# SBUF offsets of streamed matrix operands: halves of gated values at 128 bytes, the last attention group's operands at 64

## The chip, the cores and the metric

The kernel runs on one core of one Trainium2 chip. The metric is the device time of one execution in microseconds. Three executions of the kernel before took 2158.36, 2160.70 and 2164.97 us. One more execution was profiled; it took 2162.09 us, of which 2160.3 us lie between its first and its last instruction.

In the text PE is TensorE's multiplication, PEld its loading of the stationary operand, DVE is VectorE, ACT ScalarE, POOL GpSimd, and SP the engine that issues most DMAs. "Line 2125" or L2125 is a line of the kernel's source. SBUF is the on-chip memory of 128 partitions; an address in it is a number of bytes within each partition.

## The reference

One layer of a hybrid encoder over 2048 prompt tokens and 64 sample tokens, in fp32. Cut to what matters here:

```python
D_MODEL, SEQ, DEC_SEQ, D_FF, N_HEADS, HEAD_DIM = 1024, 2048, 64, 2816, 4, 128

def layer(x, ...):
    h = rmsnorm(x, g1) * (1 + sc1) + sh1
    u, q, k, v, o, gates = split(h @ w_in)          # one combined input projection
    pool_out = pool_mixer(u, ...)                   # causal pooling in 4 channel groups
    hs = mlstm_seq(q, k, v, gates, ...)             # matrix memory, 4 heads, chunks of 64
    x = x + gt1 * (concat([pool_out, gated(hs, o)]) @ w_out)
    h2 = rmsnorm(x, g2) * (1 + sc2) + sh2
    up = h2 @ w_up                                  # 1024 -> 2 x 2816
    conv = b_conv + sum(w_conv[j] * shifted(up, j) for j in range(3))
    a, g = split(conv)
    x = x + gt2 * ((silu(g) * a) @ w_down)          # 2816 -> 1024
    return x, new states
y = rmsnorm(x, g_final)
```

## The kernel before

**Arithmetic.** Every large product is made of three passes in fp32r: an operand is split into a high part (an ACT copy that rounds) and a low part (a DVE subtraction), and `PASSES` runs high x high, high x low and low x high. Values of a tile lie as `[128, 2, columns]`: the high part, then the low part. The stationary operand of a product is a block of 128 columns of a weight tile `wt`; the moving operand is a stretch of tokens. TensorE loads a stationary block before each multiplication.

**Attention part.** The 2112 tokens run in four groups of 512; the last has 576, since it takes the 64 sample tokens with it. Its normalized input is in eight tiles `hl`, the mixed output of the heads and the pooling in eight tiles `mx`. `gemm` (line 496) streams them against the weights of q, k, o, u and of the output projection: one multiplication of 512 columns for the first three groups, two of 256 and 320 columns for the last (`o.blks`). For v (line 1171) the roles are turned: blocks of `hl` are stationary and the weights move.

**Feed-forward part.** Three token groups of 704 columns (`FT`), each handled as two halves of 352 (`FH`). The up projection (line 1633) uses a scheme with seven products of half-sized blocks instead of eight; its moving operands are sums of input blocks in tiles `hx`. A pair of output rows is convolved and gated, and the gated values go to the down projection in one of two ways:

- four rows at a time through the same scheme (`Quad`, `quad_down`, line 2125): seven operands named B11, B21, B22, T1, T2, T3, T4, each half a group wide, two of them to a tile `av`. B21 with B22 and T2 with T3 are split together, 704 columns at once (`wide_hi`, line 1858 on ACT; `wide_lo`, line 1861 on DVE); the others are split alone, 352 columns at once;
- six rows plainly (`down`, line 2271): a tile `av` holds one row of 704 gated values (`split_hi`, `split_lo`), streamed as 448 and 256 columns (`ENDS`).

There are seven buffers for `av` (`AVB`); the tiles `qs`, in which weight blocks are added up, share them.

**Where the tiles lie.** Pools are stacked in SBUF from both sides, so a tile's address follows from the sizes of all that lie outside of it. All weight blocks start at a multiple of 256 bytes. In the program as built the moving operands start this far past a multiple of 256 bytes:

| Operand | Line | Columns | Bytes past |
|---|---|---|---|
| hl, mx, first three groups | 496 | 512 | 0 |
| hl, mx, last group | 496 | 256 and 320 | 128 |
| hx | 1633 | 352 | 128 |
| av, halves for quad_down | 2125 | 352 | 32 or 160 |
| av, full rows | 2271 | 448 and 256 | 160 |

For `hl` the tile's length is 18.5 times 256 bytes, so tiles start at 0 and 128 in turn, and `taken` counts along to move the operands in every second one. The stationary blocks of `hl` at line 1171 lie at 0 in the first three groups and at 128 in the last.

**Other tiles.** `fscr` gives scratch tiles of one row of 704: under the tag "rb" the row by which a normalization multiplies, under "ssum" the running sum of squares; each tag has one buffer. `final_end` finishes the last tokens; its tile `rs` is the last small one of the pool that also holds `av` and the residual rows `x0` to `x7`.

**What sets the order.** In the feed-forward part the instructions of TensorE, ACT, DVE and POOL run in the order in which the Python code issues them. Background work is cut into steps of generators (`bg`, `tick`) that are taken between multiplications; tiles are handed out in turn, and a first write into a buffer waits until the last reader of its former content is done.

Of the kernel before, what the change touches and what calls it, by code (L numbers as in the profile page):

```python
# [9 lines left out]
F32 = mybir.dt.float32  # L10
F32R = mybir.dt.float32r
AF = mybir.ActivationFunctionType
# [4 lines left out]
P = 128  # L17
# [6 lines left out]
TMAX = GT + TS  # L24
NF = 22
FT = 704
# [41 lines left out]
def tile_layer(ctx: ExitStack, tc: tile.TileContext, xT, vecs, cst, rst, w_mod, w_ada, w_qkou, w_v, w_pool,  # L68
# [73 lines left out]

    def two_parts(t, past):

        return t[:, 32 * past:32 * past + 2 * TMAX].rearrange("p (a t) -> p a t", a=2)

    def hl_tile(k, o=None):

        taken.append(1 - taken[-1])
        return two_parts(hp.tile([P, 2 * TMAX + 32], F32R, tag="hl", name=f"hl{k}"), taken[-2] ^ (o is not None and o.last))  # L150

    def mx_tile(k, o=None):
        return two_parts(mx.tile([P, 2 * TMAX + 64], F32R, tag="mx", name=f"mx{k}"), o is not None and o.last)

    x0, c0 = [[t[:, i * GT:(i + 1) * GT] for t in [big(mx_tile(k)) for k in range(4)] for i in range(2)] for _ in range(2)]

# [525 lines left out]

    def fscr(dt=F32):
        if dt in ("rb", "ssum"):
            return spare[0].tile([P, FT], F32, tag=dt, name=dt)
        return spare[0].tile([P, FT], dt, tag="fscr", name="fscr", bufs=4)


# [994 lines left out]
    def quad_sums(ds, lead=7):  # L1683

        for d in ds:
            for c in (0, 256):
                t = f2.tile([P, 2, FT], F32R, tag="av", name="qs", bufs=AVB)
                w = t.bitcast(F32).rearrange("p a t -> p (a t)")[:, :1024].rearrange("p (i c) -> p i c", i=4)
                nc.sync.dma_start(out=w, in_=w_quad[d, :, :, c:c + 256])
                for _ in range(lead):  # L1690
                    yield
                a11, a12, a21, a22 = (w[:, i] for i in range(4))
                dve.tensor_tensor(out=a22, in0=a21, in1=a22, op=ALU.add)
                yield
                dve.tensor_tensor(out=a21, in0=a11, in1=a21, op=ALU.subtract)
                yield
                dve.tensor_tensor(out=a11, in0=a22, in1=a11, op=ALU.subtract)
                yield
                dve.tensor_tensor(out=a12, in0=a12, in1=a11, op=ALU.subtract)
                yield  # L1700
                yield
                nc.sync.dma_start(out=dsum[d, :, :, c:c + 256], in_=w)
                yield
                yield

    def half_tile(nm):
        return f1.tile([P, FH], F32, tag=nm, name=nm)

    class Quad:

# [4 lines left out]
        def put(self, nm, m, part):  # L1715
            key, at = {"B11": (("a", m), 0), "T1": (("a", m), 1), "B21": (("b", m), 0), "B22": (("b", m), 1),
                       "T2": (("c", m), 0), "T3": (("c", m), 1), "T4": ("d", m)}[nm]
            if key not in self.tiles:
                self.tiles[key] = f2.tile([P, 2, FT], F32R, tag="av", name="av", bufs=AVB)
            return self.tiles[key][:, part, at * FH:(at + 1) * FH]  # L1720

        def both(self, nm, m, part):
            self.put(nm, m, part)
            return self.tiles["b" if nm == "B21" else "c", m][:, part, :]

    class Pair:

# [127 lines left out]
            return self.quad.gated[self.m, i]  # L1855

        def wide_hi(self, nm, t):
            act.activation(self.quad.both(nm, self.m, 0), t[:, :FT], AF.Copy)

        def wide_lo(self, nm, t):  # L1860
            dve.tensor_tensor(out=self.quad.both(nm, self.m, 1), in0=t[:, :FT],
                              in1=self.quad.both(nm, self.m, 0).bitcast(F32), op=ALU.subtract)

        def step_2(self):
# [42 lines left out]
                self.lo("T4", self.blocks()[2])  # L1907

        def split_hi(self):
            self.d = self.d or f2.tile([P, 2, FT], F32R, tag="av", name="av", bufs=AVB)  # L1910
            for (a, b, s) in self.o.segs:
                act.activation(self.d[:, 0, a:b], self.tg[:, a + 2 * s:b + 2 * s], AF.Copy)
            self.av[self.i] = self.d
# [70 lines left out]
    def final_end(o, x3, sums, lo, hi):  # L1984
# [3 lines left out]
        for _ in range(YA if lo == 0 else 0):  # L1988
            yield
        ps = m2_ps()  # L1990
        rs = f2.tile([P, 5], F32, tag="rs", name="rs", bufs=1) if lo > 0 else RF
        if lo > 0:
            dve.memset(ps[:, :len(tiles)], 0.0)
            yield
# [442 lines left out]
```

## Time and profile before

| What | us |
|---|---|
| Median of three executions | 2160.70 |
| The profiled execution | 2162.09 |
| Its span, first to last instruction | 2160.3 |
| PE busy | 2142.7 |
| PEld busy | 2038.7 |
| DVE busy | 1650.1 |
| ACT busy | 1101.7 |
| POOL busy | 253.8 |

The busy time of PE includes the latency of multiplications that run one behind the other, so it says that there is always one under way, not how densely they follow. A row of a group gives the line, engine, operation, the program's names of the written and read tiles, shapes and count; then the busy time in us and the mean duration of one in ns; then the idle time of the engine ahead of these instructions, with what ended most of it. A row of a timeline gives start and length in us of a run of like instructions, from the first one's start to the last one's end, and their number. A row of windows gives a stretch, its length, then for PE, PEld, DVE, ACT and POOL the busy time with the number of instructions, the granted clock, the share of the DMA engines and GB/s.

### The profile page before, as it was taken

The page shows a single profiled execution, that of the slowest core. Times are in us where ns is not written, and L with a number is a line of the kernel's source. Part 1 is how long each engine was busy: PE and PEld are TensorE (multiplying, and loading weights), DVE is VectorE, ACT ScalarE, POOL GpSimd, SP SyncE. Part 2 cuts the span into 40 slices and gives each one's busy share as a digit, 9 for nine tenths or more (in the row PEclk, how much of TensorE's full clock was granted, in tenths as well). Part 3 has the DMA queues.
Part 4 walks back from the last instruction along what each step waited for, and adds up shares of the span by engine and source line. Part 5 has one row for each costly group of instructions (what it writes and reads, how often), then busy time and mean ns, then how long its engine had stood idle before and what let it go on. Part 6 is the DMA issues. An engine that isn't in the chain of part 4 may idle for free.

```text
span 2160.3 us, 38129 instructions
## 1 busy us (share of the span) xinstructions
PE 2142.7 (99%) x13556; PEld 2038.7 (94%) x13556; DVE 1650.1 (76%) x3060; ACT 1101.7 (51%) x2192; POOL 253.8 (12%) x470
## 2 busy tenths in 40 slices
PE   8999999999999999999999999999999999999998
PEld 7888888888899999999999999999999999999998
DVE  5777768678675779788688668988886597887875
ACT  4554335234323557465556445655655364564554
POOL 0010000001000301010001110100101221121112
PEclk9999999999999999999999999999999999999999
DMA  8987997898799588797669986665668675455442
GB/s 321 326 315 237 317 324 246 282 320 274 243 298 302 196 280 307 252 336 246 233 219 314 329 299 207 235 214 205 228 222 273 218 261 182 171 180 183 172 169 85
DMA packets 296839, 541.09 MB, mean 250 GB/s; under 512 B 25760, under 2 KB 112800, under 8 KB 296648
## 3 DMA queue, kind: packets, MB, share of 16 engines
q1 hardware_dynamic: 286600, 514.13, 69.9%
q10 hardware_dynamic: 10048, 24.51, 2.9%
q8 instruction: 107, 1.75, 0.3%
q14 instruction: 84, 0.69, 0.1%
HBM read 412.56 MB, written 125.98 MB: 249 GB/s over the span
## 4 chain that ended last, share of the span: by engine, by line
PE 89%; DVE 5%; DMA 3%; issue 1%; ACT 1%; SPq 0%; POOL 0%; DVEq 0%; ACTq 0%; POOLq 0%
PE mm L1633 35%; PE mm L496 24%; PE mm L2271 10%; PE mm L2125 10%; PE mm L1171 3%; DVE wt L432 1%; DMA wt<-wsum 1%; PE m L1361 1%; PE m L1383 1%; PE m L1381 1%; PE m L1346 1%; DMA w<-w_ada 1%; DVE x L2094 1%; DVE tg L1611 1%; ACT tg L1606 0%
## 5 line engine op out<-in xcount | busy, mean ns | idle before, releaser
L1633 PE MATMUL mm<-hx,wt 128*128 128x352 f32 x5544 | 888.8, 321 | 2.2 <-DVE wt L432 1.3
L1633 PEld LDWEIGHTS mm<-hx,wt 128*128 128x128 f32 x5544 | 881.0, 188 | 4.5 <-DVE wt L432 3.2
L496 PE MATMUL mm<-hl,wt 128*128 128x512 f32 (+2 forms) x1920 | 385.3, 356 | 0.0
L432 DVE TENSOR_TENSOR wt<-raw,wt 128x512 fp32r<-128x512 f32 (+1 forms) x460 | 310.4, 681 | 75.0 <-ACT wt L429 74.9
L496 PEld LDWEIGHTS mm<-hl,wt 128*128 128x128 f32 x1920 | 314.8, 188 | 46.8 <-issue 3.6
L429 ACT ACTIVATE wt<-raw 128x512 fp32r<-128x512 f32 (+1 forms) x460 | 274.1, 603 | 163.3 <-PE mm L496 53.9
L2125 PE MATMUL mm<-av,wt 128*128 128x352 f32 x1512 | 247.4, 323 | 1.4 <-DVE x L2094 0.7
L2125 PEld LDWEIGHTS mm<-av,wt 128*128 128x128 f32 x1512 | 242.3, 188 | 4.0 <-DVE wt L432 2.0
L2271 PE MATMUL mm<-av,wt 128*128 128x448 f32 (+1 forms) x1440 | 231.3, 322 | 0.0
L2271 PEld LDWEIGHTS mm<-av,wt 128*128 128x128 f32 x1440 | 220.9, 188 | 9.7
L2094 DVE SCALAR_TENSOR_TENSOR x<-mm,MOD,x 128x352 f32<-128x352 f32 (+3 forms) x368 | 171.7, 507 | 73.3 <-PE mm L2271 58.3
L1681 ACT ACTIVATE mm<-mm 128x352 f32<-128x352 f32 x204 | 91.4, 448 | 240.9 <-PE mm L1633 177.1
L496 PE MATMUL mm<-mx,wt 128*128 128x512 f32 (+1 forms) x960 | 182.6, 352 | 0.0
L496 PEld LDWEIGHTS mm<-mx,wt 128*128 128x128 f32 x960 | 159.3, 188 | 22.5
L1611 DVE SCALAR_TENSOR_TENSOR ta<-ea,V,ta 128x704 f32<-128x704 f32 (+1 forms) x132 | 125.7, 952 | 61.3 <-ACT ta L1606 56.8
L1611 DVE SCALAR_TENSOR_TENSOR tg<-eg,V,tg 128x704 f32<-128x704 f32 (+1 forms) x132 | 125.7, 952 | 52.7 <-ACT tg L1606 50.2
L432 DVE TENSOR_TENSOR wt<-wt 128x512 fp32r<-128x512 f32 x204 | 138.8, 684 | 12.7 <-ACT wt L429 10.6
L429 ACT ACTIVATE wt<-wt 128x512 fp32r<-128x512 f32 x204 | 123.6, 621 | 31.3 <-DMA wt<-wsum 30.5
L1589 POOL COPY ea<-UC 128x2 f32<-128x2 f32 x66 | 34.7, 525 | 539.3 <-DVE ta L1611 425.3
L1829 ACT ACTIVATE tg<-tg 128x704 f32<-128x704 f32 (+1 forms) x66 | 52.5, 795 | 71.1 <-DVE tg L1611 71.1
L1171 PE MATMUL mm<-wt,hl 128*128 128x256 f32 (+1 forms) x576 | 71.2, 284 | 0.0
L1171 PEld LDWEIGHTS mm<-wt,hl 128*128 128x128 f32 x576 | 70.2, 189 | 0.8 <-issue 0.6
(315 smaller groups left out, 2204.4 us busy)
## 6 DMA issues: line engine op xcount, KB each, us to landing
wt<-wsplit SPq DMA_DIRECT2D x132, 512.0 KB, 4.3
raw<-w_up SPq DMA_DIRECT2D x198, 256.0 KB, 4.1
wt<-hl_kept SPq DMA_DIRECT2D x96, 512.0 KB, 6.0
wt<-wsum SPq DMA_DIRECT2D x132, 256.0 KB, 4.9
wsplit<-wt SPq DMA_DIRECT2D x66, 512.0 KB, 5.0
w<-w_up SPq DMA_DIRECT2D x88, 256.0 KB, 4.6
wsum<-w SPq DMA_DIRECT2D x44, 512.0 KB, 5.4
Bd<-fscr ACTq DMA_DIRECT2D x56, 352.0 KB, 3.9
```

Source lines behind the costliest of these rows:

```text
L429: act.activation(u.w[:, 0, :u.n], u.raw[:, :u.n], AF.Copy)
L432: dve.tensor_tensor(out=u.w[:, 1, :u.n], in0=u.raw[:, :u.n], in1=u.w[:, 0, :u.n].bitcast(F32), op=ALU.subtract)
L496: pe.matmul(ps[bi][:, :hi - lo], U[:, a, k % 4 * P:(k % 4 + 1) * P], mv[k][:, b, lo:hi], start=(at == 0 and pi == 0), stop=(k == order[-1] ...
L1171: pe.matmul(ps[ti][:n, :cols], h[4 * kh + k4][:, b, lo:lo + n], U[:, a, k4 % 2 * cols:(k4 % 2 + 1) * cols], start=(kh == 0 and k4 == 0 and ...
L1589: pool.tensor_copy(ext[:, 0:2], UC[:, f, :])
L1611: dve.scalar_tensor_tensor(out=t[:, :E], in0=ext[:, j:j + E], scalar=wc(j, f), in1=t[:, :E], op0=ALU.mult, op1=ALU.add)
L1633: pe.matmul(bk.t[:, :FH], U[:, a, kc * P:(kc + 1) * P], Bo.at(nm, kc, b), start=(first and kc == 0 and pi == 0), stop=(kc == 3 and pi == 2 ...
L1681: act.activation(to.t[:, :FH], bk.t[:, :FH], AF.Copy)
L1829: act.activation(self.tg[:, :E], self.tg[:, :E], AF.Silu)
L2094: dve.scalar_tensor_tensor(out=x3[n][:, a:b], in0=bk.t[:, a - lo:b - lo], scalar=gt2(n, s), in1=x3[n][:, a:b], op0=ALU.mult, op1=ALU.add)
L2125: pe.matmul(bk.t[:, :FH], U[:, a, c:c + P], quad.put(op, m, b), start=(first and m == 0 and pi == 0), stop=(m == 1 and pi == 2), skip_grou ...
L2271: pe.matmul(bks[i].t[:, :hi - lo], U[:, a, k % 4 * P:(k % 4 + 1) * P], av[k][:, b, lo:hi], start=(k == 0 and (a, b) == PASSES[0]), stop=(k ...
```

## The change

It moves operands to other addresses, and enlarges some tiles for it:

- `av` tiles become 2 x 768 columns (`HX`) instead of 2 x 704. A half starts 384 columns (1536 bytes) after the other, so both have the same place within 256 bytes. Full rows start 8 columns (32 bytes) into their part, and stay where they were within 256 bytes.
- The pool of `av` begins 32 bytes lower, because `rs` gets a second buffer that nothing else uses. With that the halves lie at 128.
- The 3584 bytes that the seven larger tiles need are partly had by giving "ssum" the tag, and so the one buffer, of "rb".
- `hl` and `mx` of the last attention group start 16 columns (64 bytes) into their tiles. For `hl` the tiles themselves still start at 0 and 128 in turn.
- The splits of B21 with B22 and T2 with T3 write, and read, two runs of 352 columns instead of one of 704.

| Operand | Bytes past a multiple of 256, before | now |
|---|---|---|
| hl, last group, moving and stationary | 128 | 64 or 192 |
| mx, last group | 128 | 64 |
| av, halves | 32 or 160 | 128 |
| av, full rows | 160 | 160 |
| hx; hl and mx of the other groups; weights | | the same |

No instruction is added, removed or moved on any engine. What changes in the order's rows is the form of the wide splits. On DVE, where the gated values of a block's second pair are split (tg is the gated value, ta its other factor, wt a weight tile being split), the kernel before has:

```order
L1837 TENSOR_TENSOR tg<-ta,tg 128x704
L1849 TENSOR_TENSOR tg<-tg 128x352 x2
L432 TENSOR_TENSOR wt<-wt 128x512
L1861 TENSOR_TENSOR av<-tg,av 128x704
L432 TENSOR_TENSOR wt<-raw,wt 128x512
L1611 SCALAR_TENSOR_TENSOR ta<-ea,V,ta 128x704 x2
L1861 TENSOR_TENSOR av<-tg,av 128x704
```

At the same place of the change stands:

```order
L1843 TENSOR_TENSOR tg<-ta,tg 128x704
L1855 TENSOR_TENSOR tg<-tg 128x352 x2
L432 TENSOR_TENSOR wt<-wt 128x512
L1867 TENSOR_TENSOR av<-tg,av 128x2x352
L432 TENSOR_TENSOR wt<-raw,wt 128x512
L1611 SCALAR_TENSOR_TENSOR ta<-ea,V,ta 128x704 x2
L1867 TENSOR_TENSOR av<-tg,av 128x2x352
```

Lines below the edits are six further down (1861 becomes 1867, 2125 becomes 2131, 2271 becomes 2277); the sequence is the same, and the two subtractions have two runs. The diff:

```diff
--- before.py
+++ after.py
@@ -142,15 +142,15 @@
 
     def two_parts(t, past):
 
-        return t[:, 32 * past:32 * past + 2 * TMAX].rearrange("p (a t) -> p a t", a=2)
+        return t[:, past:past + 2 * TMAX].rearrange("p (a t) -> p a t", a=2)
 
     def hl_tile(k, o=None):
 
         taken.append(1 - taken[-1])
-        return two_parts(hp.tile([P, 2 * TMAX + 32], F32R, tag="hl", name=f"hl{k}"), taken[-2] ^ (o is not None and o.last))
+        return two_parts(hp.tile([P, 2 * TMAX + 32], F32R, tag="hl", name=f"hl{k}"), 16 if o is not None and o.last else 32 * taken[-2])
 
     def mx_tile(k, o=None):
-        return two_parts(mx.tile([P, 2 * TMAX + 64], F32R, tag="mx", name=f"mx{k}"), o is not None and o.last)
+        return two_parts(mx.tile([P, 2 * TMAX + 64], F32R, tag="mx", name=f"mx{k}"), 16 if o is not None and o.last else 0)
 
     x0, c0 = [[t[:, i * GT:(i + 1) * GT] for t in [big(mx_tile(k)) for k in range(4)] for i in range(2)] for _ in range(2)]
 
@@ -682,7 +682,7 @@
 
     def fscr(dt=F32):
         if dt in ("rb", "ssum"):
-            return spare[0].tile([P, FT], F32, tag=dt, name=dt)
+            return spare[0].tile([P, FT], F32, tag="rb", name=dt)
         return spare[0].tile([P, FT], dt, tag="fscr", name="fscr", bufs=4)
 
 
@@ -1684,7 +1684,7 @@
 
         for d in ds:
             for c in (0, 256):
-                t = f2.tile([P, 2, FT], F32R, tag="av", name="qs", bufs=AVB)
+                t = gated("qs")
                 w = t.bitcast(F32).rearrange("p a t -> p (a t)")[:, :1024].rearrange("p (i c) -> p i c", i=4)
                 nc.sync.dma_start(out=w, in_=w_quad[d, :, :, c:c + 256])
                 for _ in range(lead):
@@ -1703,8 +1703,14 @@
                 yield
                 yield
 
+    def gated(name="av"):
+        return f2.tile([P, 2, HX], F32R, tag="av", name=name, bufs=AVB)
+
     def half_tile(nm):
         return f1.tile([P, FH], F32, tag=nm, name=nm)
+
+    def halves(t):
+        return t[:, :FT].rearrange("p (h t) -> p h t", h=2)
 
     class Quad:
 
@@ -1716,12 +1722,12 @@
             key, at = {"B11": (("a", m), 0), "T1": (("a", m), 1), "B21": (("b", m), 0), "B22": (("b", m), 1),
                        "T2": (("c", m), 0), "T3": (("c", m), 1), "T4": ("d", m)}[nm]
             if key not in self.tiles:
-                self.tiles[key] = f2.tile([P, 2, FT], F32R, tag="av", name="av", bufs=AVB)
-            return self.tiles[key][:, part, at * FH:(at + 1) * FH]
+                self.tiles[key] = gated().rearrange("p a (h t) -> p a h t", h=2)[:, :, :, :FH]
+            return self.tiles[key][:, part, at]
 
         def both(self, nm, m, part):
             self.put(nm, m, part)
-            return self.tiles["b" if nm == "B21" else "c", m][:, part, :]
+            return self.tiles["b" if nm == "B21" else "c", m][:, part]
 
     class Pair:
 
@@ -1855,10 +1861,10 @@
             return self.quad.gated[self.m, i]
 
         def wide_hi(self, nm, t):
-            act.activation(self.quad.both(nm, self.m, 0), t[:, :FT], AF.Copy)
+            act.activation(self.quad.both(nm, self.m, 0), halves(t), AF.Copy)
 
         def wide_lo(self, nm, t):
-            dve.tensor_tensor(out=self.quad.both(nm, self.m, 1), in0=t[:, :FT],
+            dve.tensor_tensor(out=self.quad.both(nm, self.m, 1), in0=halves(t),
                               in1=self.quad.both(nm, self.m, 0).bitcast(F32), op=ALU.subtract)
 
         def step_2(self):
@@ -1907,7 +1913,7 @@
                 self.lo("T4", self.blocks()[2])
 
         def split_hi(self):
-            self.d = self.d or f2.tile([P, 2, FT], F32R, tag="av", name="av", bufs=AVB)
+            self.d = self.d or gated()[:, :, 8:8 + FT]
             for (a, b, s) in self.o.segs:
                 act.activation(self.d[:, 0, a:b], self.tg[:, a + 2 * s:b + 2 * s], AF.Copy)
             self.av[self.i] = self.d
@@ -1988,7 +1994,7 @@
         for _ in range(YA if lo == 0 else 0):
             yield
         ps = m2_ps()
-        rs = f2.tile([P, 5], F32, tag="rs", name="rs", bufs=1) if lo > 0 else RF
+        rs = f2.tile([P, 5], F32, tag="rs", name="rs", bufs=2) if lo > 0 else RF
         if lo > 0:
             dve.memset(ps[:, :len(tiles)], 0.0)
             yield
```

## The prediction

> **What bounds the kernel now.** I read the page's header and busy shares first, then its chain of waits, then the groups of the matrix engine with shapes kept apart.
>
> ```profile
> span 2160.3 us, 38129 instructions
> PE 2142.7 (99%) x13556; PEld 2038.7 (94%) x13556; DVE 1650.1 (76%) x3060; ACT 1101.7 (51%) x2192; POOL 253.8 (12%) x470
> ...
> PEclk9999999999999999999999999999999999999999
> ...
> PE 89%; DVE 5%; DMA 3%; issue 1%; ACT 1%; SPq 0%; POOL 0%; DVEq 0%; ACTq 0%; POOLq 0%
> PE mm L1633 35%; PE mm L496 24%; PE mm L2271 10%; PE mm L2125 10%; PE mm L1171 3%; DVE wt L432 1%; DMA wt<-wsum 1%; PE m L1361 1%; PE m L1383 1%; PE m L1381 1%; PE m L1346 1%; DMA w<-w_ada 1%; DVE x L2094 1%; DVE tg L1611 1%; ACT tg L1606 0%
> ```
>
> TensorE is busy 99% of the span at the full granted clock, and the chain that ended last is 89% TensorE. So the time is a count of matrix multiplications times the step from one to the next. The change alters neither count nor order; it can act through that step, or through something that stops TensorE.
>
> ```profile
> L1633 PE MATMUL mm<-hx,wt 128*128 128x352 f32 x5544 | 888.8, 321 | 2.2 <-DVE wt L432 1.3 <-ACT mm L1681 0.9
> L2125 PE MATMUL mm<-av,wt 128*128 128x352 f32 x1512 | 247.4, 323 | 1.4 <-DVE x L2094 0.7 <-DVE wt L432 0.5
> L2271 PE MATMUL mm<-av,wt 128*128 128x448 f32 x720 | 157.1, 363 | 0.0
> L496 PE MATMUL mm<-hl,wt 128*128 128x256 f32 x384 | 104.5, 287 | 0.0
> L496 PE MATMUL mm<-hl,wt 128*128 128x320 f32 x384 | 102.9, 309 | 0.0
> L496 PE MATMUL mm<-mx,wt 128*128 128x320 f32 x192 | 51.2, 312 | 0.0
> L496 PE MATMUL mm<-mx,wt 128*128 128x256 f32 x192 | 51.2, 282 | 0.0
> ```
>
> The touched groups: 1512 multiplications of 352 columns at line 2125 (the halves of gated values), and in the last attention group 384 pairs of 256 and 320 columns from hl and 192 pairs from mx, 1152 multiplications. The mean in these rows (321 to 323 ns) is the latency of one; since they are pipelined, the step must come from a stretch without interruption. Weight loads show it best: one precedes each multiplication, and a stretch of n lasts n-1 steps and one load of 0.19 us. The timeline of weight loads has these:
>
> ```profile
> 1344.72 51.33 PEld L1633 LDWEIGHTS mm<-hx,wt 128*128 128x128 f32 x324
> 1107.72 23.07 PEld L2125 LDWEIGHTS mm<-av,wt 128*128 128x128 f32 x144
> 868.85 42.10 PEld L2271 LDWEIGHTS mm<-av,wt 128*128 128x128 f32 x264
> 597.78 14.45 PEld L496 LDWEIGHTS mm<-hl,wt 128*128 128x128 f32 x108
> 731.97 51.27 PEld L496 LDWEIGHTS mm<-mx,wt 128*128 128x128 f32 x384
> ```
>
> Same 352 columns, two steps: hx takes (51.33 - 0.19) / 323 = 158.3 ns, the av halves (23.07 - 0.19) / 143 = 160.0 ns. By the program as built, hx always starts 128 bytes past a multiple of 256, the halves 32 or 160 bytes past. The full rows at line 2271 (448 and 256 in turn, mean 352, at 160 bytes) take 159.4 ns. In the last attention group (mean 288 columns, at 128 bytes) hl and mx take 133.3 and 133.4 ns, but one stretch of hl is faster:
>
> ```profile
> 637.90 7.31 PE L496 MATMUL mm<-hl,wt 128*128 128x256 f32 x55
> ```
>
> This row is of multiplications, the last lasting 0.28 us: (7.31 - 0.28) / 54 = 130.2 ns, at the very offset where others take 133.3. So this stream has a short and a long rhythm at one offset, and the offset alone does not fix which.
>
> **The change part by part: halves of gated values.** All 1512 now start 128 bytes past a multiple of 256, the place of hx. With the step of hx they save 160.0 - 158.3 = 1.7 ns each, 2.6 us. Nothing has to hide this: line 2125 is 10% of the chain, and its idle time is 1.4 us in all. Bounds: the halves may keep 160.0 ns (no gain). As the other end I take the shorter hx stretch below, (22.79 - 0.19) / 143 = 158.0 ns, which gives 3.0 us. I take 2.6, since length of operand, address and weight offset are then those of the hx row.
>
> ```profile
> 1037.34 22.79 PEld L1633 LDWEIGHTS mm<-hx,wt 128*128 128x128 f32 x144
> ```
>
> The Trainium skill speaks against this term: in "SBUF — State Buffer", section "Specifications (TRN2)", the memory's lines are 16 bytes, and every offset here, old or new, is a multiple of 16; and in "TensorE: Matmul & The Clock Gate", section "Step-by-step: what each phase is for", loading the next weights takes no read bandwidth from the running multiplication. By these the address cannot matter, the 1.7 ns belong to something else about the two loops, and this term and the next are 0. The trace has no run of one loop at two offsets, so it does not decide; I keep it as the first rival.
>
> **Last attention group.** hl goes from 128 to 64 or 192 bytes (in turn), mx from 128 to 64. No row of the trace has a moving fp32r operand of this group at such a place, so I bound it by the two rhythms. Known long are the 108 of hl and 384 of mx above; known short are 55; the other 605 I leave open. If all 1152 come to the short rhythm, 3.2 ns are saved on 492 to 1097 of them, 1.6 to 3.5 us. If all come to the long one, 55 to 660 lose 3.2 ns: 0.2 to 2.1 us. I take the middle of the outer ends, -3.5 and +2.1: a gain of 0.7 us.
>
> In the same group hl is also the stationary operand of line 1171.
>
> ```profile
> 225.68 8.90 PE L1171 MATMUL mm<-wt,hl 128*128 128x256 f32 x72
> ...
> 582.09 5.85 PE L1171 MATMUL mm<-wt,hl 128*128 128x256 f32 x48
> ```
>
> At 0 bytes (an earlier group) 256 columns take (8.90 - 0.28) / 71 = 121.4 ns, at 128 (last group) (5.85 - 0.28) / 47 = 118.5. That group has 240 such multiplications, half with 256 columns, so going back to 121.4 would cost 120 x 2.9 ns = 0.35 us, and a further gain of that size would give 0.35. I take 0.
>
> **The wide splits.** The tiles are wider, so one ACT copy and one DVE subtraction of 704 columns become two runs of 352.
>
> ```profile
> L1858 ACT ACTIVATE av<-tg x36: 769/784/796, 1077.9 to 2010.9; 128x704 fp32r<-128x704 f32 x36
> ...
> L1861 DVE TENSOR_TENSOR av<-tg,av x36: 879/884/895, 1079.1 to 2013.2; 128x704 fp32r<-128x704 f32 x36
> ...
> L1845 DVE TENSOR_TENSOR av<-tg,av 128x352 fp32r<-128x352 f32 x54 | 28.2, 522 | 12.1 <-ACT av L1842 12.0
> ...
> 1853.00:1877.00 24.00, 24.00 (x150) 23.70 (x149) 22.10 (x54) 9.52 (x19) 0.00 (x0) 1.00 0.51 180
> ```
>
> The first two rows are instructions by line (shortest, median, longest ns). Below, it costs nothing more. Above, the second run costs as much as an instruction of its own: 2 x 522 - 884 = 160 ns on DVE, for 36 of them 5.8 us of DVE time. The last row is one block's down projection: TensorE 24.00 us, DVE 22.10. DVE has 1.9 us to spare, and the four subtractions of a block could add 0.64, so even the upper end is mostly covered. I take 0; without that cover the whole 5.8 us would come on top. Line 1858 on ACT (9.52 of 24.00) is further from the bound.
>
> **One slot for rb and ssum, a second rs, moved x tiles.** ssum is first written after the normalization that read rb has been drained, and rb is rewritten only after TensorE has read ssum, so nothing waits that did not wait; what is queued behind on ACT and POOL stays as it is. The tiles moved by 32 bytes are read by DVE and written by DMA, neither of which sets the end. Were a turn held up all the same, it would be once per token group, and by about the wait of a square for DVE, 1.41 us in the row below: 4.2 us for three groups. I take 0, since the order of the instructions gives no reason for it.
>
> ```profile
> 2136.95 0.58 ACT L2085 ACTIVATE fscr<-x 128x448 f32<-128x448 f32 x1 [1.41 <-DVE x L2094]
> ```
>
> **The sum.** -2.6 - 0.7 + 0 + 0 + 0 = -3.3 us. The profiled execution took 2162.1 us of which the span is 2160.3, so it would become 2158.8. That execution lies 1.4 us above the median of the three runs (2158.36, 2160.70, 2164.97); against the median I forecast 2160.7 - 3.3 = 2157.4 us.
>
> **The rivals.**
>
> *The address makes no difference.* What separates 158.3 from 160.0 is then the loop: line 1633 runs 12 multiplications into one bank, line 2125 only 6. For it speaks that at one and the same offset hl shows 130.2 and 133.3; against it that hx repeats 158.3 and 158.0 ns over 323 and 143 steps, while the halves hold 160.0 over 143. Time: 2160.7.
>
> *The last group locks to the short rhythm as well.* All of it at 130.2 ns: 3.5 us instead of 0.7, with the halves 6.1 us, so 2154.6. For it: the rhythm exists and lasted 55 multiplications. Against it: mx has held the long one for 384 without a break.
>
> *DVE becomes the bound of the down projections.* The subtraction in two runs costs a start of its own, 160 ns x 36 = 5.8 us; the block's 1.9 us of slack is not where it is needed, because the subtraction stands ahead of the weight splits at line 432 and the bank reads at line 2094, for which TensorE already waits. It decides from 72 ns per subtraction on, where 36 of them eat the 2.6 us of the halves. At its full price, and no gain in the last group: 2160.7 - 2.6 + 5.8 = 2163.9. Against it: TensorE's idle time at line 2125 is only 1.4 us, so most of that delay would have to find new waits.
>
> *The halves gain and the last group goes to the long rhythm.* 2160.7 - 2.6 + 2.1 = 2160.2.
>
> **How the numbers follow.** Forecast (halves gain, last group near its present mean) 0.40; last group short as well 0.25; no difference 0.15; last group long 0.10; DVE bound 0.10. A measurement here can tell about 0.3%, 6.5 us, from no change: faster would be under 2154.2, slower over 2167.2. Faster needs the short rhythm everywhere (2154.6) and a little more, some 0.4 of its 0.25: 0.10. Slower needs the DVE rival beyond its price or a turn held up: 0.05. The same: 0.85. The range goes from 2154.6 down and 2163.9 up by nearly the 2.3 us by which the runs of before lie below their median: 2152.5 to 2164.5.
>
> **What would show it.** In the timeline of weight loads, stretches of 144 at the halves' line should last 0.19 + 143 x 0.1583 = 22.8 us instead of 23.07; hx and line 2271's successor should stay at 158.3 and 159.4. The last group's mx stretch of 384 should last 50.1 us if short, 51.3 if long. The subtraction in two runs should stay near 884 ns, and the idle time in front of the halves' group near 1.4 us. The prediction is wrong if the halves stay at 160.0, if a stretch of the last group takes more than 133.4 per multiplication, or if TensorE waits anywhere for an operand it did not wait for before.

## The result: slower, and mostly in a group that the change does not touch

| | before | after |
|---|---|---|
| Median | 2160.77 us (15 executions, 2157.83 to 2167.48) | 2175.34 us (15 executions, 2156.48 to 2182.70) |
| Profiled execution, its span | 2162.09, 2160.3 us | 2176.46, 2174.7 us |

The ratio is 1.0059, 95% interval 1.0047 to 1.0072. The change makes the kernel slower by 0.6%, and the time lies above the predicted range. The executions also differ more among themselves than before: 26 us from the lowest to the highest instead of 10.

These are the page's busy shares and its groups with shapes kept apart, of the kernel after. Lines behind the new functions stand 6 further down, so 2131 is what 2125 was, and 2277 what 2271 was.

```profile
span 2174.7 us, 38129 instructions
PE 2156.7 (99%) x13556; PEld 2053.3 (94%) x13556; DVE 1651.1 (76%) x3060; ACT 1103.5 (51%) x2192; POOL 252.7 (12%) x470
...
PEclk9999999999999999999999999999999999999999
...
L1633 PE MATMUL mm<-hx,wt 128*128 128x352 f32 x5544 | 902.0, 323 | 2.2 <-DVE wt L432 1.2
L2131 PE MATMUL mm<-av,wt 128*128 128x352 f32 x1512 | 250.1, 324 | 0.9 <-DVE wt L432 0.6
L496 PE MATMUL mm<-hl,wt 128*128 128x256 f32 x384 | 104.2, 286 | 0.0
L496 PE MATMUL mm<-hl,wt 128*128 128x320 f32 x384 | 102.7, 309 | 0.0
L496 PE MATMUL mm<-mx,wt 128*128 128x320 f32 x192 | 50.7, 308 | 0.0
L496 PE MATMUL mm<-mx,wt 128*128 128x256 f32 x192 | 50.6, 279 | 0.0
```

Against the rows of before: the up projection, which the change leaves alone, went from 888.8 to 902.0 us (+13.2). The halves went from 247.4 to 250.1 (+2.7) instead of down. The four rows of the last group fell by 1.6 us together. That is +14.3 of the 14.4 us by which the span grew. The idle time in front of the first two groups did not grow (2.2 and 2.2, 1.4 and 0.9 us), TensorE's idle time in all hardly did (2160.3 - 2142.7 = 17.6 us, now 2174.7 - 2156.7 = 18.0), and the clock is full. One wait is new, 0.7 us for a DMA (`wt<-hl_kept`) in the first three attention groups; e1 below, with the same tiles, has none of it. So TensorE did not wait more to speak of: it stepped more slowly.

The timeline of weight loads of the kernel after (start, duration, both in us; one load precedes each multiplication) shows how:

```profile
1038.60 64.66 PEld L1633 LDWEIGHTS mm<-hx,wt 128*128 128x128 f32 x408
...
1108.93 22.83 PEld L2131 LDWEIGHTS mm<-av,wt 128*128 128x128 f32 x144
...
1259.16 55.13 PEld L1633 LDWEIGHTS mm<-hx,wt 128*128 128x128 f32 x348
1314.91 4.02 PEld L2131 LDWEIGHTS mm<-av,wt 128*128 128x128 f32 x24
1318.91 2.02 PEld L1633 LDWEIGHTS mm<-hx,wt 128*128 128x128 f32 x12
1320.91 24.02 PEld L2131 LDWEIGHTS mm<-av,wt 128*128 128x128 f32 x144
1344.91 54.02 PEld L1633 LDWEIGHTS mm<-hx,wt 128*128 128x128 f32 x324
...
1488.91 9.02 PEld L2131 LDWEIGHTS mm<-av,wt 128*128 128x128 f32 x54
1498.23 14.23 PEld L2131 LDWEIGHTS mm<-av,wt 128*128 128x128 f32 x90 [0.30 <-DVE x L2100]
1512.43 51.33 PEld L1633 LDWEIGHTS mm<-hx,wt 128*128 128x128 f32 x324
...
1861.83 21.59 PEld L2131 LDWEIGHTS mm<-av,wt 128*128 128x128 f32 x136 [0.35 <-DVE wt L432]
...
1940.40 1.30 PEld L2131 LDWEIGHTS mm<-av,wt 128*128 128x128 f32 x8
1942.05 22.62 PEld L2131 LDWEIGHTS mm<-av,wt 128*128 128x128 f32 x136 [0.36 <-DVE wt L432]
1964.65 54.02 PEld L1633 LDWEIGHTS mm<-hx,wt 128*128 128x128 f32 x324
```

With the prediction's formula (less one load of 0.19 us, by n - 1 steps) there are two steps for the same instruction at the same place. In the **short** one 144 halves take 22.83 us and 324 of hx 51.33 us, 158.3 ns each. In the **long** one they take 24.02 and 54.02 us, 166.7 ns each. Three things are to be seen. A stretch keeps the step it has: from 1314.91 to 1488.91 all of it is long, through halves and hx alike. (Between that and the short stretch at 1259.16 stand only the small multiplications of lines 739 and 740.) A wait can end it: behind the 0.30 us at 1498.23 the halves run short ((14.23 - 0.19) / 89 = 157.8 ns), and the hx after them too. And a wait can begin it: behind the 0.36 us at 1942.05 the step is (22.62 - 0.19) / 135 = 166.1 ns, and hx follows it. (The times in brackets are gaps between two loads.)

Counted over the whole trace (multiplications of 352 columns in runs of six or more whose mean step is over 164 ns, from the starts of the multiplications, steps of 200 ns and more left out), after has 2712 long ones, 1983 of them hx and 722 halves. Before has 343, of which 333 are hx and 10 halves. The 1650 more in hx, at 8.3 ns, are 13.7 us, where the row of the group gained 13.2. Of these, 1428 lie in the two chains of long stretches that begin at 1314.91 and 1942.05, 11.9 us. The other 222 come ahead of the first quad, so the halves have no part in them; their larger stretch, the 168 loads of hx at 836.64, took 28.02 us here, as long in e1's trace below, but 26.63 in e3's.

The long step was there before the change. This is one stretch of before, and two behind its halves:

```profile
1143.31 55.63 PEld L1633 LDWEIGHTS mm<-hx,wt 128*128 128x128 f32 x334 [0.58 <-DVE wt L432]
...
1321.66 23.09 PEld L2125 LDWEIGHTS mm<-av,wt 128*128 128x128 f32 x144
1344.72 51.33 PEld L1633 LDWEIGHTS mm<-hx,wt 128*128 128x128 f32 x324
```

The first, behind a wait, takes (55.63 - 0.19) / 333 = 166.5 ns; after has the same stretch, long too. But in before all nine down projections by quads hand hx over in the short step.

### The profile page after: what moved, and what is told of

Its sections match the earlier page's. It is cut to its first block, busy times and chain, and to the rows that moved or that the text cites. A ratio compares the mean times of both kernels' runs of the same rounds, so it can differ in the third digit from the quotient of the medians.

```text
span 2174.7 us, 38129 instructions
## 1 busy us (share of the span) xinstructions
PE 2156.7 (99%) x13556; PEld 2053.3 (94%) x13556; DVE 1651.1 (76%) x3060; ACT 1103.5 (51%) x2192; POOL 252.7 (12%) x470
## 4 chain that ended last, share of the span: by engine, by line
PE 58%; DVE 4%; DMA 2%; issue 1%; ACT 1%; SPq 0%; POOLq 0%; POOL 0%; ACTq 0%; DVEq 0%
PE mm L1633 37%; PE mm L2277 10%; PE mm L2131 10%; DVE wt L432 1%; DMA wt<-wsplit 1%; DMA yT<-x 1%; DVE fscr L792 0%; DVE hx L796 0%; DVE x L2100 0%; DVE tg L1611 0%; ACT tg L1606 0%; DMA wt<-dsum 0%; DVE scr L268 0%; DMA fscr<-h2d 0%; DVE ssum L527 0%
## 5 line engine op out<-in xcount | busy, mean ns | idle before, releaser
L1633 PE MATMUL mm<-hx,wt 128*128 128x352 f32 x5544 | 902.0, 323 | 2.2 <-DVE wt L432 1.2
L1633 PEld LDWEIGHTS mm<-hx,wt 128*128 128x128 f32 x5544 | 894.6, 188 | 4.0 <-DVE wt L432 2.3
L2131 PE MATMUL mm<-av,wt 128*128 128x352 f32 x1512 | 250.1, 324 | 0.9 <-DVE wt L432 0.6
L496 PEld LDWEIGHTS mm<-mx,wt 128*128 128x128 f32 x960 | 158.7, 188 | 22.6
L432 DVE TENSOR_TENSOR wt<-wt 128x512 fp32r<-128x512 f32 x204 | 139.2, 687 | 11.9 <-ACT wt L429 11.6
```

The costliest lines, as they stand in the source:

```text
L432: dve.tensor_tensor(out=u.w[:, 1, :u.n], in0=u.raw[:, :u.n], in1=u.w[:, 0, :u.n].bitcast(F32), op=ALU.subtract)
L496: pe.matmul(ps[bi][:, :hi - lo], U[:, a, k % 4 * P:(k % 4 + 1) * P], mv[k][:, b, lo:hi], start=(at == 0 and pi == 0), stop=(k == order[-1] ...
L1633: pe.matmul(bk.t[:, :FH], U[:, a, kc * P:(kc + 1) * P], Bo.at(nm, kc, b), start=(first and kc == 0 and pi == 0), stop=(kc == 3 and pi == 2 ...
L2131: pe.matmul(bk.t[:, :FH], U[:, a, c:c + P], quad.put(op, m, b), start=(first and m == 0 and pi == 0), stop=(m == 1 and pi == 2), skip_grou ...
```

## The experiments

**Theory A.** Streams 128 bytes past have two persistent steps, and halves at that place carry the long one on into hx. Halves at 32 or 160 end it. **Rivals:** something else of the change does it (larger tiles, the shared slot, the wide splits: theory B), or the last group does (theory C). Rivals D to G stand in the expectations, and a later rival H is told where it arose. All times below are against executions of before in the same series.

**e1_av160: after, with only the place of the halves put back to 160.**

```diff
-    self.tiles[key] = gated().rearrange("p a (h t) -> p a h t", h=2)[:, :, :, :FH]
+    self.tiles[key] = gated().rearrange("p a (h t) -> p a h t", h=2)[:, :, :, 8:8 + FH]
```

> The change with one edit: all halves of gated values start 160 bytes past a multiple of 256 instead of 128; tile sizes, wide splits, shared slot and the last group's 64 bytes stay. Theory A (352 columns at 128 bytes have a short rhythm of 158.3 ns and a long one of 166.7 ns, and a rhythm once taken is carried on by whatever streams on at 128; the halves at 32 or 160 had one step of 160.0 ns and brought the next stretch of hx back to the short one): the halves at 160.0 ns again, every stretch of hx right behind halves at 158.3, long stretches only behind stalls of TensorE inside hx (about 300 to 700 multiplications), time 2157 to 2162 us. Theory B (the loss is from another part: the splits in two runs, the shared slot, the moved tiles): about as slow as the change, 2170 to 2180 us.

Measured: 2161.19 us over 10 executions (2157.61 to 2171.47), ratio 1.0004 (0.9992 to 1.0017). Tiles, splits, slot and last group are those of after; 32 bytes of offset alone give the time of before again. Theory B falls. The timeline of weight loads of this kernel:

```profile
1320.72 23.08 PEld L2131 LDWEIGHTS mm<-av,wt 128*128 128x128 f32 x144
1343.77 51.34 PEld L1633 LDWEIGHTS mm<-hx,wt 128*128 128x128 f32 x324
...
1505.77 54.01 PEld L1633 LDWEIGHTS mm<-hx,wt 128*128 128x128 f32 x324
1559.75 3.88 PEld L2131 LDWEIGHTS mm<-av,wt 128*128 128x128 f32 x24
1563.60 1.93 PEld L1633 LDWEIGHTS mm<-hx,wt 128*128 128x128 f32 x12
```

Halves take 160.0 ns again. They can end the long step: behind the long stretch at 1505.77 come 24 halves, and the 12 of hx after them are short ((1.93 - 0.19) / 11 = 158 ns), with no wait between. But the long stretch itself stands right behind halves, and the hx ahead of these was short (158.1 ns from 1449.55 on), so halves at 160 can also begin the long step. That goes against the expectation, by which long stretches come only behind waits; 771 multiplications are long.

**e2_av_only: after, with hl and mx back at 128.**

```diff
-    ... name=f"hl{k}"), 16 if o is not None and o.last else 32 * taken[-2])
+    ... name=f"hl{k}"), 32 * (taken[-2] ^ (o is not None and o.last)))
-    ... name=f"mx{k}"), 16 if o is not None and o.last else 0)
+    ... name=f"mx{k}"), 32 if o is not None and o.last else 0)
```

> The change without its last-group part: hl and mx at 128 bytes as before, halves at 128. Theory A: as slow as the change, 2168 to 2182 us, with 1500 to 3500 multiplications of 352 columns at 166.7 ns, in halves and hx alike. Rival C (the last group's 64 bytes cause the loss, by the rhythm in which they hand over to the feed-forward part): 2156 to 2160 us.

**e3_last64_only: before, with only hl and mx moved to 64 and 192.**

```diff
-    return t[:, 32 * past:32 * past + 2 * TMAX].rearrange("p (a t) -> p a t", a=2)
+    return t[:, past:past + 2 * TMAX].rearrange("p (a t) -> p a t", a=2)
-    ... name=f"hl{k}"), taken[-2] ^ (o is not None and o.last))
+    ... name=f"hl{k}"), 16 if o is not None and o.last else 32 * taken[-2])
-    ... name=f"mx{k}"), o is not None and o.last)
+    ... name=f"mx{k}"), 16 if o is not None and o.last else 0)
```

> The kernel before with the last-group part alone: hl and mx of the last attention group at 64 or 192 bytes. Theory A: no long rhythm is added in the feed-forward part; the last group saves about 192 x 3.3 ns for mx, 384 x 0.5 for hl and 120 x 5 for the products with stationary hl, together 1.4 us: 2158 to 2161 us. Rival C: 2170 to 2180 us.

Measured: e2 2169.27 us (2159.40 to 2186.22, 10 executions), ratio 1.0036 (1.0010 to 1.0062); e3 2161.05 (2159.26 to 2164.26, 10), ratio 0.9997 (0.9988 to 1.0006). The halves alone make it slower, the last group alone changes nothing that can be told, so theory C falls. The profiled execution of e2 took 2186.22 us with 4025 long multiplications. Against after's that is 1313 more, at 8.3 ns 10.9 us; it was 9.8 us longer. Where the long step begins differs between these traces, which would also explain the spread of the times; only one execution of each kernel has a trace, so that is argued.

**e4_t4_at160: after, with the halves of T4 alone at 160.** T4 is the operand whose halves the quad streams last.

```diff
-    self.tiles[key] = gated().rearrange("p a (h t) -> p a h t", h=2)[:, :, :, :FH]
+    s = 8 if nm == "T4" else 0
+    self.tiles[key] = gated().rearrange("p a (h t) -> p a h t", h=2)[:, :, :, s:s + FH]
```

> The change with only the operand T4, the last 12 multiplications of each half of a down projection, at 160 bytes; the other halves stay at 128. Theory A: 12 multiplications at another offset are enough to drop the long rhythm, so hx behind halves always runs at 158.3 ns; the long one can only live inside hx behind a stall and inside one down projection: 200 to 900 long multiplications, 2156 to 2164 us. Rival D (each stretch draws its rhythm anew, nothing is carried over): hx behind the halves long about as often as in the change, 2168 to 2180 us.

Measured: 2163.19 us (2160.75 to 2170.50, 10 executions), ratio 1.0011 (1.0001 to 1.0021); 859 long. One operand in seven, moved by 32 bytes, takes back most of the loss, as theory A had it, and rival D's time (2168 to 2180 us) was not met. But one stretch of hx right behind halves (408 multiplications) is long, where theory A had none.

**e5_t4_mixed: after, with T4's two halves at 160 and 32, as in before.**

```diff
-    self.tiles[key] = gated().rearrange("p a (h t) -> p a h t", h=2)[:, :, :, :FH]
+    t = gated()
+    self.tiles[key] = (t[:, :, 8:8 + 2 * FH].rearrange("p a (h t) -> p a h t", h=2) if nm == "T4" else
+                       t.rearrange("p a (h t) -> p a h t", h=2)[:, :, :, :FH])
```

> The change, but the two halves of T4 lie at 160 and 32 bytes as before, all other halves at 128. With T4 at 160 alone hx behind the halves still fell once into the long rhythm in the trace; in the two traces with the halves at 32 and 160 in turn it never did. Theory A: the mixed places bring hx back to 158.3 ns each time, most other halves run at 158.3 or 158.4, so 2156 to 2162 us and fewer long multiplications than with T4 at 160. Rival F (which place resets is chance): like T4 at 160, 2161 to 2170 us.

Measured: 2186.44 us (2180.70 to 2189.05, 4 executions), ratio 1.0108 (1.0081 to 1.0134), the slowest of all. Theory A's number failed here, and so did rival F's. Its weight loads:

```profile
1322.88 22.89 PEld L2133 LDWEIGHTS mm<-av,wt 128*128 128x128 f32 x144
1345.74 54.02 PEld L1633 LDWEIGHTS mm<-hx,wt 128*128 128x128 f32 x324
```

The halves run short ((22.89 - 0.19) / 143 = 158.7 ns, T4's part included), and hx behind them is long, with no wait between. At the other eight quads hx comes out long too, the first in part (74 loads with a mean step of 164.1 ns). So a stream at another place does not simply end the long step: it can begin it as well, and what follows depends on how it hands over.

**Moving hx alone: h0_hx0, h32_hx32, h64_hx64, h96_hx96.** Each is e3 with hx at 0, 32, 64 or 96 bytes instead of 128; the halves stay at 32 and 160. This measures the disputed thing by itself: one loop, one count, another address.

```diff
-HX, HO = 2 * 384, 32
+HX, HO = 2 * 384, 0      # 8, 16, 24 for the others
```

> The kernel before with the last group at 64 bytes and the 5544 hx operands at 0 bytes past a multiple of 256 instead of 128; halves stay at 32 and 160. Question: which offsets have two rhythms. Theory A (rhythms come of the place of the moving operand against the weights, which lie at 0): another step than 158.3 and 166.7 ns, one value if only one rhythm exists there; for 512 columns at 0 the trace of before has 226.9 ns without change, so a single rhythm near 160 ns and 2160 to 2172 us. Rival E (the rhythms belong to the loop at line 1633, not to the address): 158.3 ns with long stretches behind stalls as before, 2157 to 2164 us.

> As the one with hx at 0, but hx at 32 bytes, one of the two places that the halves had before. Theory A: one rhythm at 160.0 ns, 2167 to 2172 us. Rival E: 158.3 ns, 2157 to 2164 us.

> As the one with hx at 0, but hx at 64 bytes. Theory A: a step of its own; by the last group's gain at 64 (mx pairs 266.7 to 263.4 ns, 1.6 ns for each multiplication) it could be as short as 157 ns in one rhythm, 2150 to 2162 us. Rival E: 158.3 ns and now and then 166.7, 2157 to 2164 us.

> As the one with hx at 0, but hx at 96 bytes. Theory A: 32 bytes off a multiple of 64 as the halves of before were, so one rhythm at 160.0 ns: hx 1.7 ns slower on 5544, 9 us, 2167 to 2172 us, and runs closer together. Rival E: 158.3 ns, 2157 to 2164 us.

One stretch of each from the timeline of weight loads; first hx at 0, then 32, 64, 96:

```profile
1344.35 52.22 PEld L1633 LDWEIGHTS mm<-hx,wt 128*128 128x128 f32 x324
```

```profile
1343.65 51.87 PEld L1633 LDWEIGHTS mm<-hx,wt 128*128 128x128 f32 x324
```

```profile
1344.02 51.87 PEld L1633 LDWEIGHTS mm<-hx,wt 128*128 128x128 f32 x324
```

```profile
1347.45 52.58 PEld L1633 LDWEIGHTS mm<-hx,wt 128*128 128x128 f32 x324
```

| hx at | Step in that stretch | Time (median, executions) | Ratio to before |
|---|---|---|---|
| 0 | 161.1 ns | 2169.64 us (6) | 1.0036 (1.0022 to 1.0050) |
| 32 | 160.0 ns | 2165.29 us (8) | 1.0025 (1.0013 to 1.0036) |
| 64 | 160.0 ns | 2165.39 us (8) | 1.0020 (1.0009 to 1.0032) |
| 96 | 162.2 ns | 2174.15 us (3) | 1.0063 (1.0040 to 1.0086) |
| 128 (e3) | 158.3 or 166.7 ns | 2161.05 us (10) | 0.9997 (0.9988 to 1.0006) |

The step follows the address, and none of these four has a long stretch (11 to 31 multiplications by the count above). So rival E falls. Theory A's numbers failed in part: at 96 bytes it had 160.0 ns, at 64 down to 157 ns, and the times at 32, 64 and 96 lie outside its ranges. The times follow the steps, though not in full: at 96 the 3.1 ns more in the mean of all hx steps would be 17 us, and 13 came. The up projection's idle time fell from 4.3 us in e3's trace to 1.0, so part of it probably stands where TensorE had waited.

**e6_hx0_w128: hx at 0, and the weights at 128.** It is e3 otherwise. If the place relative to the weights is what counts, both steps must come back.

```diff
-HX, HO = 2 * 384, 32
+HX, HO = 2 * 384, 0
-    return wp.tile([P, 2 * WN + 32], F32R, tag="wt", name="wt")[:, :2 * w].rearrange("p (a c) -> p a c", a=2)
+    return wp.tile([P, 2 * WN + 32], F32R, tag="wt", name="wt")[:, 32:32 + 2 * w].rearrange("p (a c) -> p a c", a=2)
```

> Kernel before with the last group at 64 bytes, hx at 0 bytes, and the weights at 128 bytes past a multiple of 256 instead of 0. With the weights at 0, hx at 0 had 161.0 ns (160.0 at times) and no 166.7. Theory A in its form that the place against the weights decides: the two rhythms of hx at 128 with weights at 0 return, 158.3 and 166.7 ns behind stalls, 2157 to 2165 us. Rival G (the operand's own place decides): 161.0 ns as with weights at 0, 2167 to 2171 us.

They come back. These are its weight loads, the last a stretch of the 512-column products:

```profile
842.51 28.01 PEld L1633 LDWEIGHTS mm<-hx,wt 128*128 128x128 f32 x168
...
1515.45 51.33 PEld L1633 LDWEIGHTS mm<-hx,wt 128*128 128x128 f32 x324
```

```profile
347.98 44.75 PEld L496 LDWEIGHTS mm<-mx,wt 128*128 128x128 f32 x192
```

(28.01 - 0.19) / 167 = 166.6 ns and 158.3 ns, where hx at 0 with the weights at 0 took 161.1; 659 multiplications are long, where h0_hx0 had 31. So far as this pair goes, it is the distance from weights to moving operand that sets the steps, and not the place of either. (Both at 128, which should then give 161.1 ns, was not run.) The time, 2168.70 us (2166.19 to 2172.24, 7 executions), ratio 1.0030 (1.0018 to 1.0042), is above what theory A had and inside the range of rival G, which the steps rule out. The weights of the other products moved too, and in before the stretch above took 43.52 us. By the groups the 512 columns of hl went from 276.9 to 281.6 us, those of mx from 131.3 to 134.6, the 448 of the full rows from 157.1 to 159.3: 10.2 us that have nothing to do with hx.

**The halves at the other places: e7_av192, e8_av224, then a0_av0, a32_av32, a64_av64, a96_av96.** Each is after with all halves at one other place. (For a0 it is 32 columns. For 32, 64 and 96 a changed number of `rs` buffers sets the base of the tiles as well, with the full rows kept at 160.)

```diff
-    self.tiles[key] = gated().rearrange("p a (h t) -> p a h t", h=2)[:, :, :, :FH]
+    self.tiles[key] = gated().rearrange("p a (h t) -> p a h t", h=2)[:, :, :, 16:16 + FH]   # e7; 24: e8
```

> The change with all halves at 192 bytes instead of 128, hx at 128. Theory A: the halves get the step of that place, near 160 ns, and no long rhythm of 166.7 lasts in them; hx behind them short unless the place happens to lead into the long one: 2157 to 2166 us. Rival B (the loss is from other parts of the change): 2168 to 2182 us.

> The change with all halves at 224 bytes, hx at 128. Theory A: a step of its own between 160 and 162 ns in the halves, as at 32, 96 and 160, and no long rhythm carried by them: 2157 to 2167 us. Rival B: 2168 to 2182 us.

Both times (below) lie outside theory A's ranges and inside rival B's. B is out all the same: e1 has every other part of the change and the time of before. After these two, theory A was narrowed to A2: each place of the halves has its own way of handing hx over, always the same. Rival H: places below 128 all hand over short.

> The change with all halves at 0 bytes, hx at 128. Theory A2 (the halves' place decides in which rhythm hx is entered behind them; 224 entered it long each time, 32 and 160 in turn short each time): the halves near 161 ns as hx at 0, and the stretches of hx behind them of one kind, so either 2157 to 2162 us (short) or 2174 to 2186 us (long). Rival H (only halves at hx's own place, or next to it at 192 and 224, bring the long rhythm): short, 2157 to 2163 us.

> The change with all halves at 32 bytes (before had 32 and 160 in turn). Theory A2: step 160.0 ns; hx behind of one kind, 2157 to 2162 or 2174 to 2186 us. Rival H: short, 2157 to 2163 us.

> The change with all halves at 64 bytes. Theory A2: step 160.0 ns as hx at 64; hx behind of one kind, 2157 to 2162 or 2174 to 2186 us. Rival H: short, 2157 to 2163 us.

> The change with all halves at 96 bytes. Theory A2: step 162 ns as hx at 96, which alone is 1512 x 2.0 = 3.0 us over 160.0; hx behind of one kind, 2160 to 2165 or 2177 to 2189 us. Rival H: short, 2160 to 2166 us.

| Halves at | Their mean step | Long: hx, halves | Profiled us | Median us (executions) | Ratio to before |
|---|---|---|---|---|---|
| 32/160 in turn (before) | 160.2 ns | 333, 10 | 2162.09 | 2160.77 (15) | 1 |
| 0 (a0) | 160.4 | 1095, 3 | 2167.49 | 2165.01 (8) | 1.0015 (1.0003 to 1.0026) |
| 32 (a32) | 160.1 | 375, 10 | 2160.99 | 2160.45 (8) | 0.9994 (0.9982 to 1.0005) |
| 64 (a64) | 160.0 | 2327, 44 | 2175.16 | 2172.89 (3) | 1.0053 (1.0030 to 1.0076) |
| 96 (a96) | 162.1 | 849, 15 | 2165.09 | 2165.23 (8) | 1.0017 (1.0005 to 1.0028) |
| 128 (after) | 162.4 | 1983, 722 | 2176.46 | 2175.34 (15) | 1.0059 (1.0047 to 1.0072) |
| 160 (e1) | 160.1 | 755, 12 | 2164.10 | 2161.19 (10) | 1.0004 (0.9992 to 1.0017) |
| 192 (e7) | 160.0 | 109, 18 | 2156.22 | 2171.27 (9) | 1.0044 (1.0031 to 1.0057) |
| 224 (e8) | 160.0 | 2595, 71 | 2177.52 | 2176.41 (2) | 1.0067 (1.0041 to 1.0094) |

At 224 the halves themselves hardly slow down (71 of 1512 are long), and yet nearly every stretch of hx right behind them is long. The weight loads of e8, and the same place in e7 (halves at 192) and in a64:

```profile
1318.24 23.07 PEld L2131 LDWEIGHTS mm<-av,wt 128*128 128x128 f32 x144
1341.28 54.02 PEld L1633 LDWEIGHTS mm<-hx,wt 128*128 128x128 f32 x324
```

```profile
1315.98 23.06 PEld L2131 LDWEIGHTS mm<-av,wt 128*128 128x128 f32 x144
1339.01 51.33 PEld L1633 LDWEIGHTS mm<-hx,wt 128*128 128x128 f32 x324
```

```profile
1348.08 51.33 PEld L1633 LDWEIGHTS mm<-hx,wt 128*128 128x128 f32 x324
...
1428.42 54.01 PEld L1633 LDWEIGHTS mm<-hx,wt 128*128 128x128 f32 x324
```

In all three the halves take 160.0 ns, and hx comes out long, short, or now one and now the other. Rival H falls with a64, which lies below 128 and is among the slowest. A2 holds at its ends only: of the nine stretches of hx behind the quads none is long at 32 or at 32/160 in turn, while at 224 eight of nine are, and so are all nine sets of 12 hx inside the quads; at the other places it goes either way, and the times of a0, a64 and a96 lie between or beside the ranges that A2 had. These counts are from one profiled execution of each kernel (for 32/160 in turn, e3's trace has none either). The kernel with halves at 192 shows both ends: its profiled execution, with 127 long ones, is the shortest of any kernel here (2156.22), and its median is 15 us higher.

The profiled times follow the count: from 127 long ones (e7) to 4268 (e5, profiled at 2187.45 us) are 4141 more and 31.2 us, 7.5 ns each, against the 8.3 ns between the two steps. None of these kernels is faster than before by more than can be told; a32 equals it.

**What stays open.** What decides, at a hand-over or behind a wait, which step a stream at 128 falls into. Neither the predecessor's place alone (160 hands over long at 1505.77 in e1 and short elsewhere) nor the length of the wait settles it to what the rows resolve: in after the waits shown at 1861.83 and 1942.05, for the same line, of 0.35 and 0.36 us, end in different steps ((21.59 - 0.19) / 135 = 158.5 ns and 166.1). Why streams at this distance have two steps at all was not settled either.

## Why the prediction was wrong

**What bounds the kernel** was read rightly: TensorE's steps, not waits. "It can act through that step" is how it acted.

**The halves** are the step that failed: "With the step of hx they save 160.0 - 158.3 = 1.7 ns each, 2.6 us". The place does decide the step, as e1 and the four kernels with hx moved show, and short halves took the forecast 22.8 us (22.83 at 1108.93). But 158.3 is only one of two steps at 128 bytes. I took it from two stretches of hx, both short, and did not look through the other stretches: the one of 334 quoted above, and `1143.31 55.93 PE mm L1633 x334` in the chain of waits of before, had the long one. I had seen two rhythms at one offset for hl, wrote that the offset alone does not fix which, and still gave hx and the halves one. In place of -2.6 us the halves took +2.7.

The same step hid the larger error: the sum priced only the instructions that move. The 5544 of hx run between them, at the same distance from the weights, and so share the rhythm. Before, the halves at 32 and 160 stood between two stretches of hx and, as all nine hand-overs show, left each in the short step; their 1.7 ns were the cheap price of that. Moved to 128 they carry the long step along: some 11.9 of the +13.2 us on hx. Of the prediction's own sign, "hx and line 2271's successor should stay at 158.3 and 159.4", the first half broke; the full rows stayed (264 loads in 42.10 us in both kernels).

**The last group.** Forecast -0.7, between two rhythms of 130.2 and 133.3 ns. Weight loads of after in that group, a stationary hl, then hl and mx streamed:

```profile
582.21 5.53 PEld L1171 LDWEIGHTS mm<-wt,hl 128*128 128x128 f32 x48
597.47 14.30 PEld L496 LDWEIGHTS mm<-hl,wt 128*128 128x128 f32 x108
...
731.44 50.75 PEld L496 LDWEIGHTS mm<-mx,wt 128*128 128x128 f32 x384
```

mx takes (50.75 - 0.19) / 383 = 132.0 ns and hl 131.9: one step between the two, so neither rival about this group came true. With the rows above it is 1.6 us of gain, of the forecast sign and larger. The stationary hl, now at 64 or 192 bytes, a term that the sum had at 0, gained too: 5.53 us for 48, where before took 5.77, and about 0.5 us over the nine stretches of the group (28.71 instead of 29.25 in sum), a little more than the 0.35 us that the prediction allowed:

```profile
581.97 5.77 PEld L1171 LDWEIGHTS mm<-wt,hl 128*128 128x128 f32 x48
```

e3 shows that it is too little to be measured in the time.

**The wide splits and the shared slot.** Both at 0, and right as far as the runs tell. The instructions by line, of after:

```profile
L1864 ACT ACTIVATE av<-tg x36: 771/786/797, 1079.2 to 2020.7; 128x704 fp32r<-128x704 f32 x36
...
L1867 DVE TENSOR_TENSOR av<-tg,av x36: 880/886/893, 1080.4 to 2022.9; 128x704 fp32r<-128x704 f32 x36
```

Two runs of 352 cost at most 2 ns more than one of 704 (784 to 786, 884 to 886; in e1, with the same runs, the medians are 784 and 884), not the 160 of the upper bound. e1 has all of this and equals before. So the DVE rival falls.

**The rivals.** "The address makes no difference" falls by e1 and most plainly by hx alone: 32 bytes at a time moved its step between 158.3, 160.0, 161.1 and 162.2 ns and the time by up to 0.6%. I had drawn that rival's reading from the Trainium skill too ("SBUF — State Buffer", "Specifications (TRN2)", lines of 16 bytes; "TensorE: Matmul & The Clock Gate", "Step-by-step: what each phase is for", loads that take no bandwidth from the running multiplication). The runs disagree with what I drew from it: all the offsets are multiples of 16, and e6 shows that the place of the weights counts along with that of the moving operand. None of the rivals had the hx group slower; that is the case that was missing, and why the range ended as low as it did. (2163.9 and the 2.3 us that were to be added give 2166.2, not the 2164.5 of the text; both lie below 2175.34.) Where an execution is nearly all short, the time is near the forecast of 2157.4: 2156.22 in e7's profile. The lowest of after, 2156.48, has no trace, so that it was such a one is only argued.

## What to carry to other kernels

A step read from one clean stretch is a sample, not a property: list all stretches of the group (duration by count) before using it, and look for a second value. When a change makes one stream like its neighbour, price the neighbour too, since a stream in between with a slightly longer step of its own can be what keeps the neighbour in its short one. And when executions spread widely and the clock is full, compare the steps of the same stretches before looking for a wait.

## What the runs showed of the hardware

- Multiplications of 352 fp32r columns, each with its own weight load, step at 158.3 to 166.7 ns by how far past a multiple of 256 bytes the moving operand lies, with the weights at such a multiple: 161.1 at 0, 160.0 at 32 and 64, 162.2 at 96, 158.3 or 166.7 at 128, 160.0 at 160, 192 and 224 (the last three on the halves). At 0 and 96 the halves were less even: stretches of 144 at 160.0 and 161.0 ns, and at 162.2 and 163.3. That it is the distance to the weights rests on e6 alone, and no run tested whether the period is 256 bytes.
- At 128 bytes both steps hold for hundreds of multiplications, over loop boundaries and from one group to another, until a wait or another stream comes, behind which either can follow. The times of one kernel spread accordingly (e7 from 2156.22 to 2176.88 us), though only one execution of each has a trace. The granted clock was 0.999 or 1.0 in every execution.
- The weights' place alone moved the 512-column products: with the weights at 128 instead of 0 and mx where it was, 192 loads took 44.75 us instead of 43.52, 2.8% more.
